# The squared-ReLU MLP's first product: upper and lower matmuls of a tile in blocks of eight instead of by turns

## The chip, the core and the metric

The kernel runs on one core of a Trainium2 chip. The metric is the device time of one execution in microseconds (us); the figure for a kernel is the median of its runs. Five engines of the core appear below: PE (the matrix engine; its weight loads are shown as PEld, and they overlap the matmuls), DVE (VectorE), ACT (ScalarE), POOL (GpSimd) and SP (SyncE, which issues the weight transfers here).

## The reference

The kernel computes a trunk of two layers on 256 tokens of width 2048: layer 0 has a convolution module, layer 1 a latent attention, and each layer ends with a squared-ReLU MLP. Only the MLP's first product is touched here.

```python
D_MODEL = 2048; SEQ = 256; DEPTH = 2; D_FF = 4 * D_MODEL
def rms_norm(x, g):
    xf = x.astype(jnp.float32)
    y = xf * lax.rsqrt(jnp.mean(xf * xf, axis=-1, keepdims=True) + NORM_EPS)
    return (y * g.astype(jnp.float32)).astype(x.dtype)
def sq_relu_mlp(h, w1, w2):
    return jnp.square(jax.nn.relu(h @ w1)) @ w2
...
    for layer in range(DEPTH):
        ...
        h = rms_norm(x, norm_mlp_g[layer])
        x = x + sq_relu_mlp(h, mlp_w1[layer], mlp_w2[layer])
```

All inputs and the output are float32.

## The kernel before

**Arithmetic.** A float32 product is made of matmuls in the faster `F32R` form. Each operand is split into an upper part (`hi`, the value as `F32R` holds it) and a lower part (`lo`, the rest), and three of the four partial products are summed: upper by upper, lower by upper, upper by lower. ACT makes a `hi` (line 419), DVE the `lo` that belongs to it (line 420, which reads the `hi`), both in `split_into`.

**The first product.** `xt` holds the activations, transposed, with the contraction index on the partitions: 16 blocks `k` of 128, and for each block 512 columns, 256 of the upper part (`xh(k)`) and beside them 256 of the lower part (`xl(k)`); `xhl(k)` is all 512. The weights `w1` are the stationary operand. One tile of the output is 128 of the 8192 hidden units by 256 tokens, so 64 tiles a layer and 128 in all. A tile sums in one PSUM tile of 512 columns, `ps[0]`. For each of the 16 blocks `k` there is one *upper* matmul (line 505: `wh`, the upper part of the weights, against all 512 columns, so that both "upper by upper" and "upper by lower" are made) and one *lower* matmul (line 506: `wl` against the 256 columns of `xh(k)`, added to the first 256 columns of `ps[0]`). They alternate: upper, lower, upper, lower, 32 matmuls a tile. Then ACT copies the PSUM tile out (line 511), and after every second tile DVE adds the two halves of 256 columns (line 523), and ACT and DVE square and split the result.

**Chunks.** A tile is loaded by one transfer of 1 MB (`raw`, 16 blocks of 128x128) and worked in two chunks, `h = 0` with the blocks 0 to 7 and `h = 1` with the blocks 8 to 15. Each chunk has a `prep` (one ACT and one DVE instruction of 128x1024, that is one `hi` and one `lo` buffer with eight blocks of weights) and a `run` (its 16 matmuls). `hi` and `lo` have six buffers each (`WB = 6`). `stream` writes out the order by hand: before the run of chunk n it issues the preps up to chunk n+5. So a prep waits until the buffer that it is to fill has had its last matmul, and a run waits for its own `hi` and `lo`.

**The second product.** It uses 512-column matmuls only, in threes (`mm3`, lines 194 to 196). Most of it is done by a scheme with seven products in place of eight, in units of four chunks (3, 6, 6 and 6 matmuls, 21 together), the rest by plain units of 24 matmuls.

**Order of the stages.** For each layer, 16 tiles of the first product come one after the other. Then units of the second product and tiles of the first alternate for three of the four quarters of the hidden units (`ORDERS`, T a tile, S a unit of seven, O a plain unit: `STSTSTOSTSTSTSTT` and then `TSTSTSTOSTSTSTST`), and the last quarter's second product closes the layer. Per quarter this gives 13 tiles that stand between units of the second product and one row of three tiles, so over both layers 78 single tiles, 6 rows of three, and 2 rows of 16.

Other stages that serve as yardsticks below: the convolution's pointwise product (lines 844 to 846, 256-column matmuls only), the attention's key, value and query products (lines 1408 to 1410 and 1431 to 1433, 256 columns), its scores (lines 194 to 196, 1513 and 1514, 128 and 256 columns), and its output product (lines 194 to 196, 512 columns, tile names `oh` and `ol`).

Of the kernel before, what the change touches and what calls it, by code (L numbers as in the profile page):

```python
# [20 lines left out]
KC = D // P  # L21
T = 2
S = T * P
# [58 lines left out]
def trunk_kernel(  # L82
# [26 lines left out]
    nc = tc.nc  # L109
# [28 lines left out]
    def nm(s):  # L138
        uid[0] += 1
        return f"{s}_{uid[0]}"  # L140


    def acc_tile():
        return psum["acc"].tile([P, NB], F32, tag="acc", name=nm("acc"))
# [41 lines left out]
    def rows(w, k0, nk, c0, n):  # L186

        return w[k0 * P : (k0 + nk) * P, c0 : c0 + n].rearrange(
            "(j p) n -> p j n", p=P
        )  # L190
# [127 lines left out]
    xhl = lambda k: xt[k // 4][:, k % 4, :]  # L318
    xh = lambda k: xhl(k)[:, :S]
# [95 lines left out]
    def hi_lo(n):  # L415
        return [wpool.tile([P, n, NB], F32R, tag=c, name=nm(c), bufs=WB) for c in ("hi", "lo")]

    def split_into(parts, src):
        nc.scalar.activation(parts[0], src, AF.Copy)  # L419
        nc.vector.tensor_tensor(parts[1], src, parts[0].bitcast(F32), op=ALU.subtract)  # L420
# [52 lines left out]
    def mlp(layer, ssq, next_gain, finish=None, before=None, last_w1=None):  # L473
# [5 lines left out]
        def u_tile():  # L479
            return first_tiles.pop("u", None) or mp.tile([P, 2, 2 * S], F32, tag="U", name=nm("U"), bufs=2)  # L480

        def f_tile():
            return first_tiles.pop("f", None) or mp.tile([P, 8, P], F32, tag="W", name=nm("W"), bufs=1)

        def up_units(hs, q, p, extra):

            sevens = SEVENS[layer][q]
            held = {}
            large = p in sevens or (q == PARTS - 1 and p in LATE_G[layer])

            def up_unit(b):
                ps = []

                def chunk(h):
                    def prep(raw, parts):
                        parts[h] = [a.rearrange("p a (j n) -> p (a j) n", n=P) for a in hi_lo(2)]
                        split_into(parts[h], raw[:, 8 * h : 8 * h + 8, :])

                    def run(parts):
                        if not ps:  # L500
                            ps.append(acc_tile())
                        wh, wl = parts.pop(h)
                        for j in range(8):
                            k = 8 * h + j
                            nc.tensor.matmul(ps[0], wh[:, j, :], xhl(k), start=k == 0, stop=False)  # L505
                            nc.tensor.matmul(ps[0][:, :S], wl[:, j, :], xh(k), start=False, stop=k == KC - 1)  # L506

                    def out():
                        if b == 0:
                            held["u"] = u_tile()  # L510
                        nc.scalar.activation(held["u"][:, b, :], ps[0], AF.Copy)  # L511

                    if h == 0:
                        return Chunk(prep, run)
                    return Chunk(prep, run, [add, lambda: None, square, forms, part] + extra if b == 1 else [], now=out)

                unit = Unit(rows(w1, 0, KC, ((q * NPAIR + p) * 2 + b) * P, P), KC, [chunk(h) for h in range(2)])
                unit.last_read = 1
                return unit

            def add():
                v = held["u"][:, :, :S]
                nc.vector.tensor_tensor(v, v, held["u"][:, :, S:], op=ALU.add)

            def square():
                n_s[0] += large
                v = held["u"][:, :, :S]
                nc.scalar.activation(v, v, AF.Relu)
                if p in sevens:
                    held["f"] = f = f_tile()  # L530
                    nc.scalar.activation(f[:, 0:4, :].rearrange("p (b t) n -> p b (t n)", b=2), v, AF.Square)
                    held["src"], shape, tag, n = f[:, 1:8, :], [P, 7, P], "s", N_S
                else:
                    nc.scalar.activation(v, v, AF.Square)
                    held["src"], shape = v, [P, 2, S]
                    tag, n = ("s", N_S) if large else ("g", N_G)
                held["hl"] = [mp.tile(shape, F32R, tag=tag + c, name=nm(tag + c), bufs=n) for c in "hl"]

            def forms():
                if p in sevens:  # L540
                    f = held["f"]
                    nc.vector.tensor_tensor(
                        f[:, 4:6, :], f[:, 0:1, :].broadcast_to([P, 2, P]), f[:, 1:3, :], op=ALU.subtract
                    )
                    nc.vector.tensor_tensor(f[:, 6, :], f[:, 1, :], f[:, 5, :], op=ALU.subtract)
                    nc.vector.tensor_tensor(f[:, 7, :], f[:, 3, :], f[:, 6, :], op=ALU.subtract)

            def part():
                hs[p] = held["hl"]
                split_into(hs[p], held["src"])  # L550

            if large:
                blocked[square] = lambda: n_s[0] < N_S and not (p in sevens and sums_left)
            return [up_unit(b) for b in range(2)]
# [235 lines left out]
    with ExitStack() as cx:  # L790
# [42 lines left out]
        def conv_w(n, j):  # L833
            half = raws[n].shape[1] // 2
            hi, lo = wjs[n, j // half]
            return hi[:, j % half, :], lo[:, j % half, :]
# [174 lines left out]
        with tc.manual_schedule():  # L1011
# [143 lines left out]
            for m in range(NP):  # L1155
# [4 lines left out]
                for j in range(2):  # L1160
                    k = 2 * m + j
                    wh, wl = conv_w(NU + m, j)
# [78 lines left out]
    with ExitStack() as cx:  # L1241
# [75 lines left out]
        def w_at(key, j):  # L1317
            n = pieces[key]
            half = units[n][1][1] // 2
            hi, lo = parts[n, j // half]  # L1320
            return hi[:, j % half, :], lo[:, j % half, :]
# [243 lines left out]
        with tc.manual_schedule():  # L1565
# [8 lines left out]
            ps = [[acc_tile() for _ in range(2)] for _ in range(T)]  # L1574
            for k in range(KC):
                u, j = divmod(k, 2)
# [6 lines left out]
                wh, wl = w_at(("kv", u), j)  # L1583
# [9 lines left out]
            ps = [acc_tile() for _ in range(T)]  # L1593
            for k in range(KC):
                u, j = divmod(k, 4)
# [3 lines left out]
                wh, wl = w_at(("q", u), j)  # L1599
# [55 lines left out]
            for g in range(NG):  # L1655
                for i in range(HG):
                    h = g * HG + i
# [118 lines left out]
```

## Time and profile before

| | |
|---|---|
| median of 3 runs | 1940.96 us (1940.70 to 1942.22) |
| the profiled execution: its own time | 1942.55 us |
| the profiled execution: span from the first to the last instruction | 1940.8 us |
| mean granted TensorE clock | 0.998 of full |
| upper matmuls of the first product (L505), 128 x 512 | 2048, 716.6 us busy |
| lower matmuls of the first product (L506), 128 x 256 | 2048, 574.2 us busy |
| matmuls of all stages | 10778 |
| ACT's splits in the MLP and the output product (L419) | 971 ns each |
| DVE's splits there (L420) | 1121 ns each |

How to read it: a matmul row gives the start and a modelled duration. Matmuls are pipelined, so durations overlap (392 ns for an upper one while the next starts some 230 ns later). What a matmul costs the engine is therefore the distance from its start to the next start, called a *step* below. Rows of the timeline are printed to 0.01 us; a mean step is taken over many of them, from the first start to the last.

### The profile page before, as it was taken

To read this page: it belongs to the slowest core of one execution; us is meant where nothing else is said; L and a number is where in the kernel's file an instruction comes from. 1 tells how busy PE (TensorE), PEld (TensorE's weight loads), DVE (VectorE), ACT (ScalarE), POOL (GpSimd) and SP (SyncE) were. 2 spreads that over 40 slices of the span, in tenths; PEclk is the share of its full clock that TensorE was granted. 3 is DMA by queue.
4 is the path that set the end of the run, shared out by engine and by line. 5 is a ranking of instruction groups with operands and counts; after the bars stand their busy time and mean duration, and the time that the engine had idled before them with its cause. 6 is when DMAs were issued, how large, how long until landed. Compare 5 with 4: busy or idle time off the path is not lost.

```text
span 1940.8 us, 28480 instructions
## 1 busy us (share of the span) xinstructions
PE 1915.5 (99%) x10778; PEld 1673.4 (86%) x10778; DVE 1652.4 (85%) x2372; ACT 1208.8 (62%) x1709; POOL 223.9 (12%) x184
## 2 busy tenths in 40 slices
PE   7999999999999999999999999999999999999998
PEld 7999888888888888888899998888888888888886
DVE  5999865789999999999976665657999999999887
ACT  5556654766666666666566665566766666666654
POOL 5999400000000000000001410000000000000000
PEclk9999999999999999999999999999999999999999
DMA  8666355857666667666646445765667666766663
GB/s 236 184 177 191 133 196 153 227 171 209 200 199 207 197 201 211 197 200 211 202 144 180 118 150 174 206 183 168 200 191 210 208 195 195 214 200 196 210 222 109
DMA packets 407113, 367.62 MB, mean 189 GB/s; under 512 B 15416, under 2 KB 351936, under 8 KB 406720
## 3 DMA queue, kind: packets, MB, share of 16 engines
q1 hardware_dynamic: 405952, 363.63, 62.6%
q10 hardware_dynamic: 1024, 2.17, 0.3%
q8 instruction: 84, 1.38, 0.3%
q14 instruction: 53, 0.43, 0.1%
HBM read 363.68 MB, written 2.10 MB: 188 GB/s over the span
## 4 chain that ended last, share of the span: by engine, by line
PE 95%; DVE 2%; ACT 1%; DMA 1%; POOL 1%; issue 0%; DVEq 0%; ACTq 0%; POOLq 0%
PE acc L505 24%; PE acc L194 15%; PE acc L196 15%; PE acc L195 15%; PE acc L506 12%; PE acc L846 3%; PE acc L845 3%; PE acc L844 3%; PE acc L250 1%; PE sum L894 1%; PE acc L1544 0%; POOL lo L169 0%; DMA xs<-in_x 0%; ACT hi L168 0%; PE acc L1408 0%
## 5 line engine op out<-in xcount | busy, mean ns | idle before, releaser
L505 PE MATMUL acc<-xt,hi 128*128 128x512 f32 x2048 | 716.6, 393 | 0.0
L420 DVE TENSOR_TENSOR lo<-raw,hi 128x1024 fp32r<-128x1024 f32 (+1 forms) x512 | 570.8, 1121 | 92.5 <-ACT hi L419 92.2
L506 PE MATMUL acc<-xt,lo 128*128 128x256 f32 x2048 | 574.2, 280 | 0.5 <-DVE lo L420 0.5
L419 ACT ACTIVATE hi<-raw 128x1024 fp32r<-128x1024 f32 (+1 forms) x512 | 480.3, 971 | 73.2 <-PE acc L195 67.2
L505 PEld LDWEIGHTS acc<-xt,hi 128*128 128x128 f32 x2048 | 384.4, 188 | 87.2
L506 PEld LDWEIGHTS acc<-xt,lo 128*128 128x128 f32 x2048 | 385.2, 188 | 4.1 <-DVE lo L420 0.8
L194 PE MATMUL acc<-hi,sh 128*128 128x512 f32 x930 | 364.3, 392 | 0.0
L196 PE MATMUL acc<-lo,sh 128*128 128x512 f32 x930 | 362.9, 390 | 0.0
L195 PE MATMUL acc<-hi,sl 128*128 128x512 f32 x802 | 312.3, 389 | 0.0
L168 ACT ACTIVATE hi<-raw 128x1024 fp32r<-128x1024 f32 (+2 forms) x184 | 180.0, 1005 | 47.0 <-PE acc L195 41.7
L196 PEld LDWEIGHTS acc<-lo,sh 128*128 128x128 f32 x930 | 174.6, 188 | 37.9
L194 PEld LDWEIGHTS acc<-hi,sh 128*128 128x128 f32 x930 | 174.6, 188 | 36.9
L169 DVE TENSOR_TENSOR lo<-raw,hi 128x1024 fp32r<-128x1024 f32 (+2 forms) x118 | 133.2, 1148 | 68.8 <-ACT hi L168 63.0
L419 ACT ACTIVATE hi<-V 128x1024 fp32r<-128x1024 f32 x94 | 99.6, 1059 | 129.2 <-DVE V L712 118.4
L195 PEld LDWEIGHTS acc<-hi,sl 128*128 128x128 f32 x802 | 150.7, 188 | 28.9
L946 DVE SCALAR_TENSOR_TENSOR sum<-ub,w_dw,sum 128x256 f32<-128x256 f32 x400 | 162.8, 480 | 7.6 <-ACT sum L902 6.5
L169 POOL TENSOR_TENSOR lo<-raw,hi 128x1024 fp32r<-128x1024 f32 x66 | 157.6, 2410 | 24.0 <-ACT hi L168 24.0
L419 ACT ACTIVATE hi<-T 128x1024 fp32r<-128x1024 f32 x94 | 99.4, 1057 | 89.3 <-DVE T L700 80.2
L511 ACT ACTIVATE U<-acc 128x512 f32<-128x512 f32 x128 | 76.2, 595 | 112.5 <-PE acc L506 112.0
L844 PE MATMUL acc<-xt,hi 128*128 128x256 f32 x512 | 145.3, 284 | 0.0
L845 PE MATMUL acc<-xt,hi 128*128 128x256 f32 x512 | 143.9, 281 | 1.0 <-DVE xt L207 1.0
L846 PE MATMUL acc<-xt,lo 128*128 128x256 f32 x512 | 144.0, 281 | 0.1
(270 smaller groups left out, 2797.3 us busy)
## 6 DMA issues: line engine op xcount, KB each, us to landing
raw<-in_mlp_w SPq DMA_DIRECT2D x256, 1024.0 KB, 6.2
raw<-in_conv_w_pw SPq DMA_DIRECT2D x64, 512.0 KB, 5.5
raw<-in_conv_w_pw SPq DMA_DIRECT2D x16, 1024.0 KB, 5.1
raw<-in_mla_w_o SPq DMA_DIRECT2D x16, 1024.0 KB, 5.6
raw<-in_mla_w_kv_up SPq DMA_DIRECT2D x8, 1024.0 KB, 5.5
raw<-in_mla_w_in SPq DMA_DIRECT2D x8, 576.0 KB, 3.8
raw<-in_mla_w_in SPq DMA_DIRECT2D x4, 1024.0 KB, 6.6
raw<-in_mla_w_q_up SPq DMA_DIRECT2D x16, 256.0 KB, 4.6
```

What stands on the lines that cost most here:

```text
L168: nc.scalar.activation(hi, raw[:, js, :], AF.Copy)
L169: eng.tensor_tensor(lo, raw[:, js, :], hi.bitcast(F32), op=ALU.subtract)
L194: nc.tensor.matmul(ps, sh, mh, start=start, stop=False)
L195: nc.tensor.matmul(ps, sl, mh, start=False, stop=False)
L196: nc.tensor.matmul(ps, sh, ml, start=False, stop=stop)
L419: nc.scalar.activation(parts[0], src, AF.Copy)
L420: nc.vector.tensor_tensor(parts[1], src, parts[0].bitcast(F32), op=ALU.subtract)
L505: nc.tensor.matmul(ps[0], wh[:, j, :], xhl(k), start=k == 0, stop=False)
L506: nc.tensor.matmul(ps[0][:, :S], wl[:, j, :], xh(k), start=False, stop=k == KC - 1)
L844: nc.tensor.matmul(o, wh[:, bs], xh(k), start=k == 0, stop=False)
L845: nc.tensor.matmul(o, wh[:, bs], xl(k), start=False, stop=False)
L846: nc.tensor.matmul(o, wl[:, bs], xh(k), start=False, stop=k == KC - 1)
```

## The change

A chunk no longer alternates. In the chunk `h = 0` all eight upper matmuls come first and then all eight lower ones; in the chunk `h = 1` the eight lower ones come first and then the eight upper ones. A tile thus runs eight upper, sixteen lower, eight upper. The same 32 matmuls are made with the same operands; the one that opens the sum (`start`) is still the upper matmul of block 0, the one that closes it (`stop`) is now the upper matmul of block 15 instead of the lower one. No transfer, split, buffer or other instruction is added or taken away.

```diff
                         wh, wl = parts.pop(h)
-                        for j in range(8):
-                            k = 8 * h + j
-                            nc.tensor.matmul(ps[0], wh[:, j, :], xhl(k), start=k == 0, stop=False)
-                            nc.tensor.matmul(ps[0][:, :S], wl[:, j, :], xh(k), start=False, stop=k == KC - 1)
+                        for low in (h, 1 - h):
+                            for j in range(8):
+                                k = 8 * h + j
+                                if low:
+                                    nc.tensor.matmul(ps[0][:, :S], wl[:, j, :], xh(k), start=False, stop=False)
+                                else:
+                                    nc.tensor.matmul(ps[0], wh[:, j, :], xhl(k), start=k == 0, stop=k == KC - 1)
```

## The prediction

> **What bounds the kernel now.** I read first the page (shares of the engines, chain of work that ended last), then the waits of PE, then the timeline of single matmuls.
>
> ```profile
> span 1940.8 us, 28480 instructions
> ...
> PE 1915.5 (99%) x10778; PEld 1673.4 (86%) x10778; DVE 1652.4 (85%) x2372; ACT 1208.8 (62%) x1709; POOL 223.9 (12%) x184
> ...
> PE 95%; DVE 2%; ACT 1%; DMA 1%; POOL 1%; issue 0%; DVEq 0%; ACTq 0%; POOLq 0%
> ...
> L505 PE MATMUL acc<-xt,hi 128*128 128x512 f32 x2048 | 716.6, 393 | 0.0
> ...
> L506 PE MATMUL acc<-xt,lo 128*128 128x256 f32 x2048 | 574.2, 280 | 0.5 <-DVE lo L420 0.5
> ```
>
> PE is the bound: 95% of the chain that ended last is matmuls, and the two groups that the change reorders, 4096 matmuls, waited 0.5 us in all. So a transfer or a split can hardly gain or lose anything by itself. What counts is the step, the distance from one matmul's start to the next, and whether it depends on what stands beside it. One tile between two units of the second product:
>
> ```profile
> 601.19 0.39 PE L196 MATMUL acc<-lo,sh 128*128 128x512 f32 x1
> 601.41 0.40 PE L505 MATMUL acc<-xt,hi 128*128 128x512 f32 x1
> 601.65 0.28 PE L506 MATMUL acc<-xt,lo 128*128 128x256 f32 x1
> 601.76 0.39 PE L505 MATMUL acc<-xt,hi 128*128 128x512 f32 x1
> ...
> 606.96 0.40 PE L194 MATMUL acc<-hi,gh 128*128 128x512 f32 x1
> ...
> 608.59 0.39 PE L195 MATMUL acc<-hi,gl 128*128 128x512 f32 x1
> ```
>
> From 601.76 to 606.96 lie 15 pairs: 0.3467 us for an upper and a lower matmul. The whole tile takes 606.96 - 601.41 = 5.55 us.
>
> Now the same two widths, each among its own kind. First row and last row of a stretch of 512-column matmuls (86 steps lie between), and of one of 256-column matmuls (170 steps):
>
> ```profile
> 930.01 0.39 PE L194 MATMUL acc<-hi,sh 128*128 128x512 f32 x1
> ...
> 949.50 0.39 PE L196 MATMUL acc<-lo,sh 128*128 128x512 f32 x1
> ```
>
> ```profile
> 100.04 0.28 PE L845 MATMUL acc<-xt,hi 128*128 128x256 f32 x1
> ...
> 120.13 0.28 PE L845 MATMUL acc<-xt,hi 128*128 128x256 f32 x1
> ```
>
> 19.49 / 86 = 0.2266 us and 20.09 / 170 = 0.1182 us, together 0.3448. The alternating pair costs 0.3467, some 2 ns more. The difference is small but occurs 2048 times, and the change trades 32 turns a tile for two.
>
> **The change part by part.**
>
> *Steps inside the blocks.* Sixteen upper steps at 0.2266 are 3.626 us. For the lower step there are two rows of the trace at the same width: 0.1182 above, and the attention's key product, 23 steps from first row to last:
>
> ```profile
> 1045.59 0.28 PE L1408 MATMUL acc<-kvh,hi 128*128 128x256 f32 x1
> ...
> 1048.27 0.28 PE L1410 MATMUL acc<-kvh,lo 128*128 128x256 f32 x1
> ```
>
> 2.68 / 23 = 0.1165. I take 0.118, nearer the long row, which has the same `xt` operand: sixteen are 1.888 us. The far bound below is the scores' 128-column matmuls (three steps between these rows):
>
> ```profile
> 1096.49 0.28 PE L195 MATMUL acc<-kTh,qTl 128*128 128x128 f32 x1
> ...
> 1096.83 0.28 PE L1514 MATMUL acc<-kpB,qpB 128*128 128x128 f32 x1
> ```
>
> 0.113 with half the columns: at this width something other than the columns sets the step, so a run of lower matmuls cannot go below it by much. What weighs here is that each matmul brings its own 128 columns of weights. The Trainium skill (TensorE: Matmul & The Clock Gate, LDWEIGHTS) puts such a load at 128 / 1.2 = 107 ns, whatever the rows; by that rule, which speaks against the change, a lower matmul's load loses the cover of a 227 ns upper matmul and must fit under a neighbour of 118 ns; it would still fit, with 11 ns to spare, and the sum would stand. The rows of 113 ns at half the width agree with a floor near there.
>
> *Turns.* Two are left. Upper to lower: the first upper step of the tile above, 601.41 to 601.65, is 0.005 us longer by my reading of the fine starts than the later ones (0.24 printed, against 0.23); I take +0.005. Lower to upper: 512-column matmuls behind narrower ones do not start at 0.2266. In the tile above the seven steps from 606.96 to 608.59 take 1.63 where 7 x 0.2266 = 1.586: 0.04 us lost, and this the old order pays too wherever a unit of the second product follows. Behind a few pure 256-column matmuls the loss has two sizes:
>
> ```profile
> 1155.84 0.39 PE L194 MATMUL acc<-hi,oh 128*128 128x512 f32 x1
> ...
> 1157.00 0.39 PE L196 MATMUL acc<-lo,oh 128*128 128x512 f32 x1
> ```
>
> ```profile
> 1166.21 0.40 PE L194 MATMUL acc<-hi,oh 128*128 128x512 f32 x1
> ...
> 1168.53 0.39 PE L195 MATMUL acc<-hi,ol 128*128 128x512 f32 x1
> ```
>
> Five steps in 1.16 (0.027 over) and ten in 2.32 (0.054 over). I take 0.033, nearer the first and the 0.04 of the tile; bounds 0.025 and 0.054. It is now paid inside the tile, by the second eight upper matmuls, and no longer by the unit behind it.
>
> So a new tile is 3.626 + 1.888 + 0.005 + 0.033 = 5.552 us, wherever it stands.
>
> *Tiles by place.* (a) 78 single tiles, the last of each of the 6 rows of three, and the last of layer 0's row of 16, 85 together: before 5.55 + 0.04 = 5.59, saved 0.038 each, 3.2 us. (b) Tiles with another tile behind them, 12 in the rows of three and 12 of layer 0's first row: 5.55 to 5.552, nothing. (c) Some tiles run in a slower rhythm, all 16 that open layer 1 and the first 3 of layer 0:
>
> ```profile
> 1299.76 0.40 PE L505 MATMUL acc<-xt,hi 128*128 128x512 f32 x1
> ...
> 1305.41 0.40 PE L505 MATMUL acc<-xt,hi 128*128 128x512 f32 x1
> ```
>
> 16 pairs in 5.65 us, 0.353 a pair. In layer 0 this rhythm ends at the stall quoted next, and single tiles do not have it: it lasts while nothing breaks the alternation. The blocks break it twice a tile, so I count it as gone: 5.654 - 5.552 = 0.10, times 19, 1.9 us. Bounds: 0 if it stays in another form, 2.5 us if the blocks run at their best.
>
> *The one stall.* It stands in the fourth tile of layer 0, first chunk:
>
> ```profile
> 335.83 1.22 DVE L420 TENSOR_TENSOR lo<-raw,hi 128x1024 fp32r<-128x1024 f32 x1 [1.27 <-ACT hi L419]
> 336.18 2.00 ACT L419 ACTIVATE hi<-raw 128x1024 fp32r<-128x1024 f32 x2
> 336.26 0.40 PE L505 MATMUL acc<-xt,hi 128*128 128x512 f32 x1
> 337.11 0.39 PE L506 MATMUL acc<-xt,lo 128*128 128x256 f32 x1 [0.46 <-DVE lo L420]
> 337.26 2.36 DVE L420 TENSOR_TENSOR lo<-raw,hi 128x1024 fp32r<-128x1024 f32 x2 [0.20 <-ACT hi L419]
> 337.34 0.39 PE L505 MATMUL acc<-xt,hi 128*128 128x512 f32 x1
> ```
>
> The upper matmul had its `hi`; the lower one waited for the `lo`, ready at 337.05. The step is 0.85 and the next 0.23, against 0.23 and 0.12: 0.73 us lost. In blocks eight upper matmuls come first, so the lower part is wanted at 336.26 + 8 x 0.227 = 338.08, and the stall is gone: 0.7 us. What is late next is the second chunk, which begins with lower matmuls: 338.08 + 8 x 0.118 = 339.02. Its `lo` is the first of the two that end at 337.26 + 2.36 = 339.62, so ready near 338.45: half a microsecond to spare.
>
> *Waits in the steady part.* In a second chunk the lower part is wanted one upper step, 0.23 us, earlier than now. One of the tightest:
>
> ```profile
> 523.56 3.49 DVE L420 TENSOR_TENSOR lo<-raw,hi 128x1024 fp32r<-128x1024 f32 x3
> ...
> 526.32 0.39 PE L505 MATMUL acc<-xt,hi 128*128 128x512 f32 x1
> 526.55 0.28 PE L506 MATMUL acc<-xt,lo 128*128 128x256 f32 x1
> ```
>
> The `lo` of this chunk is the first of three, ready at 523.56 + 1.2 = 524.8; wanted at 526.55 before, at 526.3 after: 1.5 us of cover left. If it were gone, the lower matmuls would hold the queue and all of the tile behind them, for as long as DVE is late. In the first chunk of a tile the lower part is wanted 1.6 us later than now, which only helps. Buffers: in the first chunk `hi` is free after eight matmuls and not with the last but one; in the second it is free one lower step, 0.12 us, later, with over a microsecond in hand. I count all of this at nothing. The copy out of PSUM (L511) waits for the tile's last matmul as before, and that comes no later.
>
> *Sum.* 3.2 + 0 + 1.9 + 0.7 = 5.8 us off the profiled execution, whose own time is 1942.55 us (1.75 more than its span): 1936.75. That execution lies 1.6 us above the median of the runs, so against the median 1940.96 - 5.8 = **1935.1 us**. With the lower step at 0.1165 and the turn at 0.025 a tile is 5.52, the terms become 85 x 0.07 + 24 x 0.03 + 19 x 0.13 + 0.7 = 9.8: 1931. With the turn at 0.054 and 0.1182 it is 5.576, and they become 1.2 - 0.6 + 1.5 + 0.7 = 2.8: 1938.
>
> **The rivals.**
>
> *The order is indifferent.* Each matmul pays for its own columns, and the sum of a tile is the same in blocks; the 2 ns are what two different stages make of one step, and the 0.04 behind a tile remains. For it: the slower of the two 256-column rows leaves only 2 ns of 347. Against it: the longer first step and the seven long steps behind a tile, which depend on the neighbour. Only the stall goes: 1940.96 - 0.7 = 1940.2 us, or 1938.4 if the slow rhythm goes too. The Trainium skill (TensorE: Matmul & The Clock Gate, Back-to-back issue gap) has such a rule: N / 2.4 + 2.5 ns for N columns, 216 and 109, a function of a matmul's own width. The rows here are 10 ns above both and vary with the place, so it is borne out in kind alone.
>
> *Slower: the upper blocks fall into a slow rhythm.* 512-column matmuls among themselves are not always at 0.2266. In the attention's first product (52 steps between these rows) they stay at 12.14 / 52 = 0.2335 for the whole stretch, with no wait:
>
> ```profile
> 1022.35 0.40 PE L196 MATMUL acc<-lo,xt 128*128 128x512 f32 x1
> ...
> 1034.49 0.40 PE L194 MATMUL acc<-hi,xt 128*128 128x512 f32 x1
> ```
>
> If every turn from lower to upper throws PE into this rhythm and eight or sixteen matmuls are too few to leave it, a tile is 16 x 0.2335 + 1.888 + 0.005 = 5.629: 0.039 more for 85 tiles, 0.079 for 24, 0.025 less for 19, and 0.7 less for the stall: 3.3 + 1.9 - 0.5 - 0.7 = +4.0, 1945.0 us. It decides from an upper step of about 0.231 on (16 x 0.0024 = 0.038 eats the saving of a single tile). For it: the ten long steps quoted at 1166.21. Against it: both quoted turns settle within ten steps.
>
> *Lower blocks at the floor.* At 0.113 a step a tile saves 16 x 0.005 = 0.08 more, 10 us over 128 tiles: 1925 us. Against it: both 256-column rows.
>
> *New waits.* DVE is busy 85% of the span, and the gain could be given back as waits for `lo` in second chunks: about the time before, 1941 us. Against it: the 1.5 us of cover.
>
> **How the numbers follow.** The forecast 0.60; the indifferent order 0.20; the slow rhythm 0.10; the floor 0.05; new waits 0.05. A measurement of this kernel tells about 0.2%, 3.9 us, from no change: faster is below 1937.1, slower above 1944.8. The forecast's own range is 1931 to 1938, a small part of it above 1937.1. Faster: 0.57 + 0.05 = 0.62. Slower: the slow rhythm, 0.10. The same: the rest, 0.28. The range takes in the forecast and the indifferent order and leaves out the slow rhythm and the floor: 1931 to 1941.
>
> **What would show it.** In the profile after: upper steps of 0.227 and lower of 0.117 to 0.118 inside the blocks, a tile of 5.52 to 5.58 us, the units of the second product at 0.2266 from their first matmul, layer 1's first 16 tiles no longer at 5.65, and no wait of L506 near 337. The forecast is wrong if upper steps stay above 0.23 through a block, if lower steps in a row reach 0.12, or if PE shows waits for `lo` in second chunks.

## The result, and the profile after

The changed kernel takes 1946.04 us (1945.90 to 1946.13), the kernel before beside it 1942.10 us (1940.65 to 1943.93): a ratio of 1.0021, 95% interval 1.0012 to 1.0030. The change makes the kernel slower by about 4 us, where 6 us less was forecast.

The page of the changed kernel (L509 is now the upper matmul, L507 the lower one):

```profile
span 1944.2 us, 28476 instructions
...
PE 1919.3 (99%) x10778; PEld 1675.2 (86%) x10778; DVE 1652.7 (85%) x2372; ACT 1206.4 (62%) x1709; POOL 223.9 (12%) x184
...
PE 96%; DVE 1%; ACT 1%; POOL 1%; DMA 1%; issue 0%; DVEq 0%; ACTq 0%; POOLq 0%
...
L509 PE MATMUL acc<-xt,hi 128*128 128x512 f32 x2048 | 512.8, 396 | 0.0
...
L507 PE MATMUL acc<-xt,lo 128*128 128x256 f32 x2048 | 262.5, 281 | 0.0
```

The span grew by 3.4 us and PE's busy time by 3.8 us. PE is still the bound, and neither group waited at all. (The busy time of a group counts overlapping durations once, so it fell with the grouping; it says nothing on the cost.) PE's waits for other engines, in full:

```profile
PE tr L290 <- DMA stage<-in_conv_b_dw: 12.0, 1, 12.0
PE sum L897 <- DVE ub L872: 1.1, 1, 1.1
PE acc L1538 <- DVE pr L1532: 1.1, 2, 1.0
PE acc L848 <- DVE xt L207: 1.0, 1, 1.0
PE acc L1136 <- DVE cn L1126: 0.3, 1, 0.3
PE tr L250 <- DVE xn L1038: 0.2, 1, 0.2
```

The wait of the lower matmul for its `lo` near 337 is gone, and neither MLP group waits in its place (the 0.2 us at L250 is a transpose outside the MLP's products). So the 4 us lie in the steps themselves. The timeline of a single tile; rows of the same line that follow each other are merged now, with their count:

```profile
602.06 0.39 PE L196 MATMUL acc<-lo,sh 128*128 128x512 f32 x1
602.28 2.03 PE L509 MATMUL acc<-xt,hi 128*128 128x512 f32 x8
604.15 2.05 PE L507 MATMUL acc<-xt,lo 128*128 128x256 f32 x16
606.03 2.02 PE L509 MATMUL acc<-xt,hi 128*128 128x512 f32 x8
607.90 0.40 PE L194 MATMUL acc<-hi,gh 128*128 128x512 f32 x1
...
608.58 0.39 PE L194 MATMUL acc<-hi,gh 128*128 128x512 f32 x1
```

From the starts: eight upper steps in 1.87 us, 0.2338 each; sixteen lower steps in 1.88, 0.1175 each; eight upper steps in 1.87 again. The whole tile takes 5.62 us where it took 5.55. (These starts are printed to 0.01 us; over the 78 single tiles the three parts take 1.869, 1.884 and 1.861 us on average, so an upper step is 0.2336 and 0.2327.) The first eight upper matmuls are as slow as the last eight, though no lower one stands before them, and the second product behind the tile is at 0.227 from the first step on (607.90 to 608.58, three steps).

The stages, each from its first matmul to the next stage's first (the last one to the end of the span), from the profiled executions, and beside them the mean of the 78 single tiles and what the twelve matmuls behind such a tile take over 12 x 0.22667:

| us | before | after | difference |
|---|---|---|---|
| to the first MLP | 318.57 | 318.54 | 0.0 |
| MLP of layer 0 | 675.83 | 677.89 | +2.06 |
| attention | 261.19 | 261.20 | 0.0 |
| MLP of layer 1 | 685.18 | 686.61 | +1.43 |
| one single tile | 5.552 | 5.614 | +0.062 |
| behind a single tile | 0.035 | 0.006 | -0.029 |
| a row of three tiles | 16.645 | 16.867 | +0.222 |

The second product also follows the six rows of three, and loses 0.029 less there too: 78 x 0.062 + 6 x 0.222 - 84 x 0.029 = 4.8 + 1.3 - 2.4 = +3.7 us. The opening rows of 16 tiles, from their first matmul to the second product's first, went from 90.53 to 90.77 us in layer 0, where the stall and the three slow tiles are gone, and from 91.17 to 90.76 in layer 1: 0.2 less together. The matmuls behind these two rows give back 0.1 more. That makes the 3.5 us of the two MLPs.

### The profile page after: what moved, and what is told of

The parts are those of the page before. It is cut to its first block, busy times and chain, and to the rows that moved or that the text cites. A ratio compares the mean times of both kernels' runs of the same rounds, so it can differ in the third digit from the quotient of the medians.

```text
span 1944.2 us, 28476 instructions
## 1 busy us (share of the span) xinstructions
PE 1919.3 (99%) x10778; PEld 1675.2 (86%) x10778; DVE 1652.7 (85%) x2372; ACT 1206.4 (62%) x1709; POOL 223.9 (12%) x184
## 4 chain that ended last, share of the span: by engine, by line
PE 96%; DVE 1%; ACT 1%; POOL 1%; DMA 1%; issue 0%; DVEq 0%; ACTq 0%; POOLq 0%
PE acc L509 25%; PE acc L194 15%; PE acc L195 15%; PE acc L196 15%; PE acc L507 12%; PE acc L849 3%; PE acc L848 3%; PE acc L847 3%; PE acc L250 1%; PE sum L897 1%; PE acc L1547 0%; POOL lo L169 0%; DMA xs<-in_x 0%; ACT hi L168 0%; PE acc L1411 0%
## 5 line engine op out<-in xcount | busy, mean ns | idle before, releaser
L509 PE MATMUL acc<-xt,hi 128*128 128x512 f32 x2048 | 512.8, 396 | 0.0
L509 PEld LDWEIGHTS acc<-xt,hi 128*128 128x128 f32 x2048 | 375.6, 188 | 79.3
L507 PEld LDWEIGHTS acc<-xt,lo 128*128 128x128 f32 x2048 | 260.2, 188 | 11.7
L507 PE MATMUL acc<-xt,lo 128*128 128x256 f32 x2048 | 262.5, 281 | 0.0
L849 PE MATMUL acc<-xt,lo 128*128 128x256 f32 x512 | 144.0, 281 | 0.0
```

The costliest lines, as they stand in the source:

```text
L849: nc.tensor.matmul(o, wl[:, bs], xh(k), start=False, stop=k == KC - 1)
```

## The experiments

The question was why an upper matmul behind an upper one takes 0.2338 us here and a matmul of the same width 0.2267 in the second product. One difference does not show in any view, since no trace prints addresses: by a reading of the built program, which no run records, a block of `xt` starts 32 bytes past a multiple of 64, while the weights' buffers `hi` and `lo` and the second product's operands start on multiples of 64. The padding `PAD_RIGHT` behind `xt` sets this. The runs below move `xt` by 32 bytes, and the matmuls alone set the distance themselves.

**Theory A**: the distance of the two operands' addresses sets the step. **Theory B**: upper matmuls in a row are slow because each brings two new operands. **Theory C**, the prediction's slow rival: the turn from lower to upper throws PE into a slow rhythm.

### Blocks, with `xt` 32 bytes further on

```diff
-PAD_RIGHT = 48
+PAD_RIGHT = 40
```

> The changed order, with the padding that lies behind xt cut from 48 to 40 floats, so that every block of xt starts 32 bytes later, on a multiple of 64 bytes (before: 32 past one). Theory A (address): an upper matmul that follows an upper one pays about 6.7 ns, 16 columns' worth, because its 2048 bytes of xt start in the middle of a 64-byte line, and the alternating order hides that. Then upper steps fall from 0.2334 to about 0.2267, a single tile from 5.63 to about 5.52, and the time lies at 1926 to 1934 us, below before; the convolution's 256-column steps and the attention's first product (0.2334) should fall as well. Theory B (operands): upper matmuls in a row are slow because each brings both a new stationary and a new moving operand, where the second product keeps one of them. Then upper steps stay at 0.233 and the time at 1944 to 1947 us. Theory C (rhythm): the turn from lower to upper throws PE into a slow rhythm. It says the same as B for this run, but the steps should depend on what stands before the block.

Measured: 1940.60 us, before beside it 1940.89; ratio 0.9995 (0.9986 to 1.0004). A single tile in the timeline:

```profile
602.60 1.98 PE L509 MATMUL acc<-xt,hi 128*128 128x512 f32 x8
604.41 2.08 PE L507 MATMUL acc<-xt,lo 128*128 128x256 f32 x16
606.32 2.00 PE L509 MATMUL acc<-xt,hi 128*128 128x512 f32 x8
608.16 0.39 PE L194 MATMUL acc<-hi,gh 128*128 128x512 f32 x1
```

The first eight upper steps are 1.81 / 8 = 0.226 us. The order is the same, the operands are as new as before, and only the address moved: B and C fall, and A holds for the upper step. In the attention's first product, where `xt` is the stationary operand, the 512-column step fell as well, from 0.2333 to 0.2285. The last eight take 1.84, 0.03 over 8 x 0.2267: with this distance there is a turn to pay, about what the prediction took. The lower steps went up to 1.91 / 16 = 0.119. The convolution's 256-column steps, which were expected to fall, rose from 0.1183 to 0.1199 (steps without a wait), and the stages up to the first MLP from 318.54 to 320.65 us: 256-column matmuls are slower with the distance 0. The turn, the lower steps and the convolution are why the time missed the 1926 to 1934 us expected; the MLPs fell to 674.49 and 683.10.

### By turns, with `xt` 32 bytes further on

The same line, in the kernel before.

> The order of before (upper and lower by turns), with the same cut of the padding, xt on multiples of 64 bytes. Theory A: the alternating pair hides the cost, so it stays near 0.3467 in the MLP and only the other stages gain: 1936 to 1940 us; if the pair too falls, to about 0.343, some 1928 us. Theories B and C: no change of the steps, 1940 to 1943 us.

Measured: 1951.91 us; ratio 1.0056 (1.0044 to 1.0069). No theory had said this. First matmul of a single tile, and first behind it:

```profile
606.08 0.39 PE L505 MATMUL acc<-xt,hi 128*128 128x512 f32 x1
...
611.71 0.40 PE L194 MATMUL acc<-hi,gh 128*128 128x512 f32 x1
```

16 pairs in 5.63 us, 0.352 a pair: by turns, the distance that is best for the upper blocks gives nearly the slow rhythm of 0.353. So the place of `xt` suits one order or the other. At the old distance turns win (1942.1 against 1946.0), at the distance 0 blocks win (1940.6 against 1951.9). Of the 11 us that turns lose by the move, 2 lie ahead of the first MLP (318.57 to 320.54 us).

### The steps alone

A kernel of nothing but matmuls, in which the moving operand starts m bytes and the stationary one s bytes past a multiple of 64 (this kernel and the two like it below ran once each):

```diff
+    def block(name, m, s, order, n_mov=8):
+        ps = psum.tile([P, 512], F32, tag="acc", name=name)
+        for i, (low, k) in enumerate(order):
+            a = m // 4 + (k % n_mov) * 512
+            b = s // 4 + (k % 16) * P
+            n = S if low else 512
+            w = wlo if low else wup
+            nc.tensor.matmul(
+                ps[:, :n], w[:, b : b + P], mov[:, a : a + n], start=i == 0, stop=i == len(order) - 1
+            )
+        return ps
```

> Matmuls alone, with no work on the other engines and no waits; the rest of the computation is left out. Blocks of 48 upper steps (512 columns), 64 lower steps (256 columns), 32 pairs by turns, and three tiles in blocks of 8, 16 and 8, each with the moving operand m bytes and the stationary operand s bytes past a multiple of 64; every matmul brings new operands, except in the last block, where all read the same moving operand at m = 32. Theory A: upper steps of 0.2267 at m0_s0 and 0.2334 at m32_s0, the same 0.2334 in the block that reads one moving operand, pairs by turns near 0.3467 in both. Theory B: 0.2334 at m0_s0 and at m32_s0 alike, and 0.2267 in the last block. Theory C: 0.2267 in all blocks of upper steps alone, 0.233 only inside the tiles in blocks.

The view of stretches shows from, to, their length, and PE's busy time with the instructions in it, then the granted clock, the DMA's share and its GB/s; each stretch runs from a block's first start to the next block's, and counts the last matmul before it as well. The first four are 48 upper matmuls with m, s = 0, 0; 32, 0; 0, 32; 32, 32:

```profile
25.16:36.04 10.88, 10.88 (x49) 1.00 0.01 2
36.04:47.24 11.20, 11.20 (x49) 1.00 0.00 0
47.24:58.44 11.20, 11.20 (x49) 1.00 0.00 0
58.44:69.35 10.91, 10.91 (x49) 1.00 0.01 2
...
114.17:121.85 7.68, 7.68 (x65) 1.00 0.01 2
121.85:129.39 7.54, 7.54 (x66) 1.00 0.00 0
129.39:136.96 7.57, 7.57 (x66) 1.00 0.01 2
256.54:267.50 10.96, 10.96 (x48) 1.00 0.01 1
...
189.44:206.15 16.71, 16.71 (x98) 1.00 0.01 1
222.96:239.83 16.87, 16.87 (x97) 1.00 0.00 1
```

10.88 / 48 = 0.2267, then 0.2333, 0.2333 and 0.2273 with both operands moved alike, whose last eight steps are at 0.2266: it is the distance between the two that counts, not the place of either. So the reason that was put on record with theory A, the moving operand's start in the middle of a 64-byte line, falls; its forecast for the upper step holds. The next three stretches are 64 lower matmuls at 0, 0; 32, 0; 0, 32: 0.1200, 0.1178, 0.1183, the other way round. The next is the block with one and the same moving operand at 32, from its first start to its last (47 steps): 0.2332, so new operands are not the cause (B). With no other engine at work the distance still sets the upper step. The last two stretches are three tiles each in blocks of 8, 16 and 8, at 0, 0 and at 0, 32: 5.57 and 5.62 us a tile, as in the kernel with `xt` moved (5.567 on average) and in the changed kernel (5.614). With m at 16 and 4 bytes and s at 0 the upper step was 0.232 and 0.235, with s at 16 and m at 0 it was 0.233. Turns took 0.347 a pair at 0, 0 and at 32, 0, but 0.353 at 0, 32 and at 32, 32, which has the distance 0 as well.

### One layer only

```diff
         xt[:] = [
             pool.tile([P, KC // NNB, 2 * S], F32R, name=nm("xt")) for _ in range(NNB)
         ]
+        if name == "xt0":
+            pool.tile([P, 8], F32, name="pad_xt0")
```

with `PAD_RIGHT = 40`, so that the padding of 32 bytes returns in layer 0 alone.

> The changed order; xt keeps its place through layer 0 (32 bytes past a multiple of 64) and lies on a multiple of 64 in layer 1's MLP alone. If the distance of the two operands' addresses sets the upper step, the two MLPs of one program part: layer 0 keeps 0.2334 and its span of 677.9 us, layer 1 has 0.2267 and 683.1 us where the changed kernel has 686.6; the time is 1942 to 1943 us. If something else of the earlier run with moved xt made the gain (the convolution or the attention that moved with it), layer 1 stays at 0.233 and the time at 1944 to 1946 us.

Measured: 1942.62 us (before 1942.26; ratio 1.0003, 0.9994 to 1.0013). A tile of layer 0 and a tile of layer 1, in one execution (L511 upper, L509 lower):

```profile
602.27 2.03 PE L511 MATMUL acc<-xt,hi 128*128 128x512 f32 x8
604.14 2.04 PE L509 MATMUL acc<-xt,lo 128*128 128x256 f32 x16
...
1618.09 1.98 PE L511 MATMUL acc<-xt,hi 128*128 128x512 f32 x8
1619.90 2.08 PE L509 MATMUL acc<-xt,lo 128*128 128x256 f32 x16
```

1.87 against 1.81 for eight upper steps. The spans are 677.92 and 683.08 us, as expected to 0.1: `xt`'s place in layer 1 alone makes the difference there.

### Runs of other lengths, alone

The same matmul kernel with 64 pairs in runs of 1, 2, 4, 8 and 16.

> Matmuls alone, the rest of the computation is left out: 64 upper and 64 lower ones in runs of 1, 2, 4, 8 and 16, with xt's stand-in 0 or 32 bytes off the weights, each behind 24 aligned upper matmuls; and runs of 1 behind four kinds of lead (upper or lower, 0 or 32 bytes off). If a misaligned upper matmul pays only behind another upper one, a pair at 32 bytes goes up with the run length: 0.3467 at 1, about 0.349 at 2, 0.350 at 4, 0.351 at 8 and 16 (0.2333 + 0.118). If by turns all is hidden by any lower neighbour, a run of 2 is already at 0.3467. At 0 bytes a pair is 0.3467 in runs (0.2267 + 0.120) whatever their length, plus the turn. Runs of 1 have two rhythms, 0.3467 and 0.3533: if the lead chooses, the four leads differ at one and the same distance of addresses; if the addresses choose, they don't.

Runs of 1 and of 2 at m = 32:

```profile
169.89:192.09 22.20, 22.20 (x129) 1.00 0.00 1
197.55:219.75 22.20, 22.20 (x129) 1.00 0.00 1
```

22.20 / 64 = 0.3469 a pair both times, so a run of two hides the cost here as turns do; from the same trace runs of 4, 8 and 16 took 0.350, 0.351 and 0.350. At m = 0 the five were 0.353, 0.348, 0.350, 0.349 and 0.347. Runs of 1 at m = 0 took 0.353 behind three leads and 0.347 behind lower matmuls at 32 bytes; at m = 32 all four gave 0.347. So for runs of 1 both the distance and what went before decide.

### Runs of two and of four in the kernel

```diff
+                        for k0 in range(8 * h, 8 * h + 8, 2):
+                            for low in range(2):
+                                for k in range(k0, k0 + 2):
+                                    j = k - 8 * h
...
```

> xt where it is in the kernel before (32 bytes past a multiple of 64), a chunk as two upper, two lower, two upper, two lower and so on. With matmuls alone a pair in runs of two took 0.3467 us at that distance, as by turns. If this holds in the kernel, a single tile takes 5.55 us as before the change, and the time is 1938 to 1941 us, the lower end if the slow rhythm of layer 1's first tiles and the stall of layer 0 go. If every upper matmul behind an upper one pays its 6.7 ns, half of them pay: 2048 / 2 x 6.7 ns = 6.9 us over the kernel before, 1947 to 1949 us.

Measured: 1952.63 us, ratio 1.0052 (1.0037 to 1.0067): the first forecast failed, and the second was too low. A tile (L510 upper, L508 lower):

```profile
604.22 0.63 PE L510 MATMUL acc<-xt,hi 128*128 128x512 f32 x2
604.69 0.39 PE L508 MATMUL acc<-xt,lo 128*128 128x256 f32 x2
604.92 0.63 PE L510 MATMUL acc<-xt,hi 128*128 128x512 f32 x2
...
609.85 0.40 PE L194 MATMUL acc<-hi,gh 128*128 128x512 f32 x1
```

Two pairs take 0.70 us, the tile 5.63, and the second product behind it loses 0.063 us, more than behind turns (0.035).

> The same with runs of four. Alone, a pair took 0.3500 us at this distance, 3.3 ns over turns: 2048 x 3.3 ns = 6.8 us more, less what the slow rhythm, the stall and the long steps behind a tile give back (up to 5 us): 1942 to 1947 us, near the changed kernel. If only whole blocks of eight pay, it is 1938 to 1941 us like runs of two.

Measured: 1944.99 us, ratio 1.0015 (1.0005 to 1.0025), in the range of the first forecast; single tiles 5.607 us. So runs of four are long enough to pay, and runs of two are worse still.

### The sign of the distance

The stretch of matmuls alone had 0.3469 for runs of two, the kernel 0.352. In the kernel, by the same reading of the built program, `xt` lies 32 bytes behind the weights' place, in that experiment 32 bytes ahead.

> Matmuls alone again, the rest of the computation is left out, now with the moving operand 32 bytes behind the weights' place in a line and not ahead of it, as xt and the weights of this kernel lie (0 against 32, and 96 against 0, which is the same modulo 128), in runs of 1, 2, 4, 8 and 16, then runs of 1 behind four leads, and upper matmuls with 64 bytes between the operands. If the sign of the distance explains the miss of the runs of two, a pair in runs of two takes about 0.352 us here as in the kernel (0.3467 with the operand ahead), and runs of 1 show the slow rhythm of 0.3533; if it does not, both are 0.3467 again. Upper matmuls at 64 bytes take 0.2267 if the period of the effect is 64 bytes.

Runs of 1, 2, 4 and 8 at 0, 32, then runs of 1 behind upper matmuls at m = 32, then upper matmuls 64 bytes apart:

```profile
30.62:53.22 22.60, 22.60 (x129) 1.00 0.00 1
58.69:81.17 22.48, 22.48 (x129) 1.00 0.00 1
86.65:109.10 22.45, 22.45 (x129) 1.00 0.00 1
114.58:137.09 22.51, 22.51 (x129) 1.00 0.00 1
338.88:361.07 22.19, 22.19 (x129) 1.00 0.00 1
411.96:422.72 10.76, 10.76 (x49) 1.00 0.00 0
```

A pair takes 0.3531, 0.3513, 0.3508 and 0.3517: with the kernel's sign the runs of two and of eight come within 1 ns of the kernel's 0.352 and 0.351 (5.63 / 16 and 5.614 / 16), which explains the miss from 0.3467. It does not explain which of the two is dearer: alone it is the runs of eight, in the kernel the runs of two. Runs of 1 have the slow rhythm behind aligned matmuls, upper or lower, and behind lower ones at 32 bytes, and the fast one (22.19 / 64 = 0.3467) behind upper matmuls at 32 bytes. In the kernel before, however, the single tiles stand behind the second product's steps of 0.2267 and are fast, so this does not settle what picks the rhythm there. The last stretch is 10.76 / 47 = 0.2289, neither 0.2267 nor 0.2333: the effect's period is not 64 bytes. The other pair of places with the same sign, 96 and 0, gave 0.350 for runs of 1 and 0.353 for the longer ones, so the distance alone does not settle every figure of a mixture.

### A version that beats both

The changed order, with `xt` at its old place for the convolution and on multiples of 64 from the first MLP on: the layer experiment's edit and one line more.

```diff
+        open_xt("xt0m")
         ssq, add, prepare = residual_stage(True, g_mlp[0])
```

> The changed order, with xt 32 bytes past a multiple of 64 in the convolution as before and on a multiple of 64 from layer 0's MLP on (xt is opened once more there). From the stages of the runs so far: convolution as before, MLP of layer 0 674.5 and of layer 1 683.1 us, the attention's first product 0.6 less: 4.0 us off the kernel before, 1936.5 to 1937.5 us. If the convolution does not mind (its loss in the run with moved xt came from something else), 1938 to 1939 us; if the order alone costs the 5 us, 1944 us or more.

Measured: 1938.56 us (1938.39 to 1938.66), before beside it 1942.26; ratio 0.9981, interval 0.9973 to 0.9990. That is 0.2%, but each of its runs is below every run of the kernel before (1940.57 to 1943.81). From its page:

```profile
span 1936.8 us, 28476 instructions
...
PE 1912.1 (99%) x10778; PEld 1678.4 (87%) x10778; DVE 1651.9 (85%) x2372; ACT 1204.8 (62%) x1709; POOL 223.9 (12%) x184
```

4.0 us less span than before, in the stages that were expected: MLPs 674.43 and 683.08, attention 260.62, and 318.71 up to the first MLP, so the convolution keeps its time. The median lies above the 1936.5 to 1937.5 us expected, which were counted from the 1940.9 of the earlier runs of the kernel before. It falls into the range of the second forecast by luck only, for the convolution does mind: it lost 2 us when its `xt` was moved. Both halves are needed: the order alone costs 4 us, the address alone (by turns, the convolution's 2 us included) costs 11.

## Why the prediction was wrong

**The step that failed** is the first term, "Sixteen upper steps at 0.2266 are 3.626 us". The row for it came from the second product, whose operands start on multiples of 64 bytes alike; the upper matmul's do not. Measured at the old address: 0.2336 and 0.2327 in the two blocks, the prediction's own sign of being wrong (above 0.23 through a block). Sixteen took 3.730 us, 0.104 more a tile and 13 us over 128 tiles. The lower steps took 1.884 for 1.888, and the 0.038 for the turns did not come, so the tile is 5.552 + 0.104 - 0.004 - 0.038 = 5.614 us: 0.062 too much, 7.9 us over 128 tiles, of the 9.3 us between the 5.8 forecast off the span and the 3.5 measured on it. The row that would have been right stood in the text, as the rival's: 0.2335 in the attention's first product, the one stretch of 512-column matmuls with `xt` as an operand (the stationary one there). It was priced but read as a rhythm of PE, not as a property of the operands; it should have been preferred because it shares a tensor with the change.

**The slower rival** had the size: +4.0 forecast, +3.9 measured. Its mechanism is not the one: it asked for a turn that throws PE off, and the first eight upper matmuls of a tile, behind a unit of the second product at 0.227, are at 0.2336 from the first on. The threshold given with it, an upper step of 0.231, does not follow from its own working, 0.2266 + 0.0024 = 0.229.

**Lower steps**: 0.118 forecast, 0.1175 measured. Right; the row preferred for it had the same `xt` operand.

**The turns.** The upper matmuls behind the lower ones lost nothing further at the old address (1.87 us like the first eight); at the distance 0 they lose 0.03, the value taken. What the prediction moved from the second product into the tile did leave the second product: 0.035 us behind a single tile before, 0.006 after.

**The slow rhythm of layer 1's opening tiles.** It was counted as gone, at 0.10 us a tile. The rhythm did go, but the blocks there cost nearly as much:

```profile
1301.51 3.89 PE L509 MATMUL acc<-xt,hi 128*128 128x512 f32 x16
1305.24 2.06 PE L507 MATMUL acc<-xt,lo 128*128 128x256 f32 x16
1307.14 3.89 PE L509 MATMUL acc<-xt,hi 128*128 128x512 f32 x16
```

5.63 us a tile against 5.65. Its saving may also have been set against the wrong base: the profiled execution lay 1.6 us above the median of three runs (0.45 above that of the eleven run beside the changed kernel), and 16 x 0.10 = 1.6 is just what the slow rhythm costs there. The times of the kernel before, in all its runs, stand mostly in groups near 1940.8, 1942.2 and 1943.7, those of each kernel in blocks of eight within 0.4 us; rows of turns that fall into the one rhythm or the other would do that. That is argued from the size, since only one execution of the kernel before has a trace.

**Waits and the stall**: right. The stall is gone, and DVE's splits stayed ahead although second chunks want their `lo` earlier.

**The indifferent order** falls too: at the distance 0 or 32 a matmul's step depends on its neighbour, by up to 6 ns a pair. The Trainium skill's rule by the matmul's width alone (TensorE: Matmul & The Clock Gate, Back-to-back issue gap: 216 ns for 512 columns, given there for an isolated matmul) meets 227, 229 and 233 ns here for one and the same width, according to the distance of the addresses; the measurement decides.

**What stays open**: why a distance of 32 bytes costs an upper step 6.7 ns and gives a lower one 2 ns back, why turns hide it, what its period is, and what picks the rhythm of turns.

## What to carry to other kernels

Before the step of one stage is used to price another, compare the operands' start addresses as well as their widths, and not modulo 64 alone (0.2289 us at 64 bytes against 0.2267 at 0): the order of matmuls and the place of their operands are one choice, and an address tuned for one order can be wrong for the other. A row that shares a tensor with the change is a better yardstick than a longer row with other tensors. And when a reordering loses a few nanoseconds a matmul, try it again with one operand moved by 32 bytes before dropping it.

## What the runs showed of the hardware

A stream of 512-column matmuls, each with its own 128 x 128 weights, takes 0.2267 us a step at the distance 0 between the starts of moving and stationary operand (m and s both 0; 0.2273 with both at 32), 0.2333 when they are 32 bytes apart, either way round, and 0.2289 at 64 bytes. For 256 columns it is 0.1200 at the distance 0 and 0.1167 to 0.1183 at 32. Alternating the two widths has two stable rhythms, 0.3467 and 0.3533 us a pair, at the same addresses, with no wait and the clock at 1.00. At the distance 0, and with the moving operand 32 bytes behind, the matmuls in front decided between them alone; with it 32 bytes ahead all four leads gave 0.347. A rhythm lasted for 64 pairs alone and for 16 tiles in the kernel.
